# Gated DeltaNet stage: U and transposed W prepared per chunk, the outputs in their own stream, and one block inversion per group

## The chip, the cores and the metric

One core of one Trainium2 chip runs the whole program in one launch. The metric is device time in microseconds (us) of one execution; smaller is better. "Before" is the kernel as it stood, "after" the changed one.

## What is computed

Two layers of a backbone work on 256 context and 256 latent tokens of width 2048. Layer 0 is a bidirectional chunked gated DeltaNet with 16 key heads and 32 value heads, layer 1 a differential attention. The change is in layer 0 alone (and in buffer counts that both layers share). For one chunk of a value head the reference is

```python
lower = jnp.where(strict, jnp.einsum('nbhid,nbhjd->nbhij', kb, kc) * decay, 0.0)
tinv = lax.linalg.triangular_solve(eye + lower, eye, left_side=True, lower=True, unit_diagonal=True)
u = tinv @ (vc * bc[..., None])
w = tinv @ (kb * jnp.exp(gc)[..., None])
def step(s, inp):
    v_new = u_i - w_i @ s
    o_i = q_i @ s + a_i @ v_new
    s = s * gl_i[..., None, None] + jnp.einsum('bhck,bhcv->bhkv', k_i, v_new)
```

Each direction walks over the chunks; the state `s` is carried from step to step, while `tinv`, `u`, `w` and `a_i` depend on no state.

## The kernel before

Tokens lie in four chunks of 128 (two of context, two of latent tokens; a "half" is a pair of them). A group `g` (16 of them) is one key head with its two value heads. Every group needs six projections of 128 columns (q, k, v0, v1, z0, z1), each 16 x 3 matmuls of 512 columns with a weight split into a high and a low part: `raw_tile` loads 128x512 floats by a DMA of the SP queue, ACT casts the high part (L185), POOL or DVE subtracts for the low part (L187). All later stages load their weights through the same `raw_tile` ring (tag `raw`, 4 buffers).

The order of the DeltaNet stage is written by a small planner (`Drive`): generators ("streams") yield their cost on the matmul engine, events or buffer counts, and of the streams that are ready the one of lowest priority number goes on. A scheduler of the framework then places the instructions on the engines' queues; on the chip each queue is in order. The streams are

- `filler` (priority 9): the projections, in the order z0 g, z1 g, q g+1, v0 g+1, v1 g+1, k g+2. What follows a projection (`post_k`, `post_q`, `post_v`, `post_z`) makes the convolution on DVE (L472) and transposes.
- `stream_m` (6): for each half the matrix `ma` (L687 to L748) from a product of the keys and the decay; `grm` is loaded by DMA (L681), scaled by four DVE instructions, exponentiated by ACT. Then `block_inv` (L698): the half's 8 matrices go to memory (`mb_d`), come back as 64 blocks of 16x16 on 64 partitions (`bk`), are inverted row by row with 15 pairs of DVE instructions (`bP` L712, `bY` L714) and go back through `tu_d`.
- `stream_lev` (1.5, two of them): three doubling levels (L777 to L802) from the 16x16 blocks to the inverse `uf` of the whole chunk, with PSUM tag `iv`, DVE result `R` (L783) and ACT casts.
- `stream_at` (5): the decayed product of queries and keys `at`, with loads `gra`.
- `stream_b` (1): four steps t per group, both directions in each. `steps_b` (L849) is one serial chain: keys times state (`sb`), `y` on DVE (L874), a bf16 cast `yb` on ACT (L879), `uf` times `yb`, cast `x0`, `m16` and `ml` times `x0`, a residual on DVE (L905), `uf` times it, `x` (L911), `kx` times `x`, the new state `S` (L918, L921); and in the same step the output `O` from queries times state and `at` times `x`, PSUM tag `so` with one buffer.
- `chain_fin` (2): norm, transposes back and gate `sz` of the outputs. `stream_ada` (7): modulation vectors on POOL and ACT (L138, L139) with loads `aw` and `cr`.

After the groups follow the output projection (`woA`, `woB`), layer 1 with values `dv`, keys `dk`, queries `dq`, gates `dg` for 8 heads, and its output projection `dwo`. Queries, gates and `dwo` have 256 columns per matmul, all else 512.

Of the kernel before, what the change touches and what calls it, by code (L numbers as in the profile page):

```python
# [61 lines left out]
def body(ctx, tc, D, d, out):  # L62
# [87 lines left out]
    def ada_pieces(lcs):  # L150
# [78 lines left out]
    mb_d = [dram.tile([8, US], F16, name=f"mb_d{i}") for i in range(2)]  # L229
    tu_d = [[dram.tile([8, US], F16, name=f"tu_d{i}{j}") for j in range(2)] for i in range(2)]  # L230
# [21 lines left out]
    gq = lambda: pt_("gq", 1)  # L252
# [4 lines left out]
    def so():  # L257
        return psm.tile([P, 2, 2, P], F32, tag="so", name="so", bufs=1)
# [37 lines left out]
    for k0 in range(0, KT, SK):  # L296
        with tc.high_priority():
            for kind in range(2):
                if k0 + kind:
                    pr = kind * HKT + k0 // 2  # L300
                    ada_pair(0, pr, ada_load(0, pr, t0, "ar", 12), (gq, tr)[np_ % 2](), t0)
                np_ += 1
# [24 lines left out]
    lv = cst.tile([P, 3, P], F32, name="lv")  # L327
    nc.sync.dma_start(lv, d["consts"][:, C_LV + 4 * P:C_LV + 7 * P].rearrange("p (l i) -> p l i", l=3))
# [37 lines left out]
    hh = lambda kt: hhi[:, kt, :]  # L366

# [7 lines left out]
    def gates():  # L375
        class t1:
            @staticmethod
            def tile(shape, dt, name, tag, bufs=2):
                return dl.tile(shape, dt, name="gt_" + name, tag=tag, bufs=dict(at=3, x=1, cy=1, jk=1, y=1, grm=1, gra=1, ma=1).get(tag, bufs))
# [53 lines left out]
        g = t1.tile(sh, F32, name="g", tag="x")  # L433
# [57 lines left out]
    def ev(*k):  # L491
        return evs.setdefault(k, Event())

    res = {k: Res(n) for k, n in dict(pj=2, th=2, kT=3, qT=3, v=3, sz0=2,
                                      sz1=2, gq=1, m=4, uf=8, at=3).items()}
# [59 lines left out]
    def post_k(g, ps):  # L555
# [27 lines left out]
        sts[g].update(kT=kT, ktok=kt_)  # L583
        yield 0.87, 1.5 * LX
        dr.set("kT", g)

    def post_q(g, ps):
# [13 lines left out]
        yield 0.0, 9.0 * LX  # L601
        pq = tr()
# [5 lines left out]
        dr.set("rq", g)  # L608
        yield 0.85, 0.0
# [13 lines left out]
    def post_v(g, h, ps):  # L623
        if h == 0:
            yield ("v", 2)
            sts[g]["v"] = [dl.tile([P, 2, 2, P], F32, tag="v", name=f"v{g}{i}", bufs=3) for i in range(2)]
# [9 lines left out]
        v = sts[g]["v"]  # L636
        pv = tr()
# [54 lines left out]
    def scaled(o, gr, pg, s, nm):  # L692
        gm = dl.tile([P, 2, P], F32, tag="gm", name=f"gm{s}{nm}", bufs=1)
        nc.vector.tensor_tensor(gm, pg.unsqueeze(1).to_broadcast([P, 2, P]), gam[:, s], ALU.mult)
# [3 lines left out]
    def block_inv(g, half, m16):  # L698
        par = half
        nm = f"{g}{half}"  # L700
        nc.sync.dma_start(full(mb_d[par]), m16.rearrange("p d c h i -> p (d c h) i"))
        bk = dl.tile([64, 16, 16], F16, tag="bk", name=f"bk{nm}", bufs=1)
# [592 lines left out]
```

## Time and profile before

| | |
|---|---|
| median of 3 runs | 3165.09 us (3162.82 to 3166.16) |
| the profiled execution | 3170.24 us, its span 3168.5 us |
| busy: PE, DVE, ACT, POOL | 89%, 62%, 59%, 64% |
| mean granted clock of TensorE | 0.954 |

PE is the matmul engine, DVE VectorE, ACT ScalarE, POOL GpSimd, SP the queue that issues nearly all DMAs. A busy share of PE counts a matmul until its result is written, so that PE can be 89% busy and still not be issuing at its peak. The page cuts the span into slices: the DeltaNet stage is about the first two thirds (to some 2130 us), the output projection lasts to some 2447 us, layer 1 fills the rest. In the first stage all four engines are half to nine tenths busy, in the last one PE alone is.

### The profile page before, as it was taken

How to read it: one execution, taken by the hardware profiler on the slowest of the kernel's cores; microseconds unless marked ns; L12 is line 12 of the kernel's file. 1: busy time of each engine (PE TensorE's matmuls, PEld its weight loads, DVE VectorE, ACT ScalarE, POOL GpSimd, SP SyncE). 2: the span in 40 equal slices, each digit the busy share in tenths (PEclk: the TensorE clock that was granted, in tenths of full speed). 3: DMA queues.
4: the chain of work that ended last, by engine and by line, in shares of the span. 5: the costliest groups of instructions: out<-in, count | busy, mean ns of one | idle time of the engine just before them, and what ended most of it. 6: DMA issues, size and time to landing. Idle time of an engine off the chain costs nothing.

```text
span 3168.5 us, 52448 instructions
## 1 busy us (share of the span) xinstructions
PE 2833.0 (89%) x16178; PEld 2236.6 (71%) x16178; DVE 1980.1 (62%) x4274; ACT 1863.0 (59%) x5466; POOL 2026.2 (64%) x2370
## 2 busy tenths in 40 slices
PE   4977888888998988998988988899898999999998
PEld 1555666676776766776766766677686888888888
DVE  2148768778778688588688688632334664545454
ACT  3545666666766766766666666654455665434354
POOL 2567677777787777777777777566466677322234
PEclk6988999999999999999999999999999999999999
DMA  9645445455545555545455546656744454333345
GB/s 362 223 114 118 123 119 135 123 133 118 139 134 129 127 126 133 128 129 136 122 125 131 132 118 134 173 171 189 230 147 132 144 164 150 123 110 113 117 127 164
DMA packets 511795, 457.06 MB, mean 144 GB/s; under 512 B 241684, under 2 KB 383764, under 8 KB 511508
## 3 DMA queue, kind: packets, MB, share of 16 engines
q1 hardware_dynamic: 511508, 453.68, 51.8%
q8 instruction: 127, 2.08, 0.3%
q14 instruction: 156, 1.28, 0.1%
q10 hardware_dynamic: 4, 0.02, 0.0%
HBM read 427.18 MB, written 26.36 MB: 143 GB/s over the span
## 4 chain that ended last, share of the span: by engine, by line
PE 33%; DVE 26%; DMA 19%; ACT 7%; POOL 7%; issue 5%; SPq 2%; POOLq 0%; DVEq 0%; ACTq 0%
PE pj L83 28%; DMA gra<-gc_d 5%; POOL rp L138 4%; DMA grm<-gc_d 4%; DVE bP L712 4%; DVE grm L687 3%; DMA aw<-in_adaw_dram 3%; DVE gra L687 2%; DVE bY L714 2%; ACT rp L139 2%; DVE R L783 1%; PE sb L83 1%; DMA ar<-in_adaw_dram 1%; PE iv L83 1%; DVE ma L695 1%
## 5 line engine op out<-in xcount | busy, mean ns | idle before, releaser
L139 ACT ACTIVATE rp<-rp 128x256 f32<-128x256 f32 x1024 | 426.9, 417 | 378.6 <-POOL rp L138 375.5
L712 DVE TENSOR_TENSOR bP<-bX,bY 64x1 f32<-64x1 f32 (+14 forms) x480 | 228.8, 477 | 18.1 <-ACT bY L710 9.8
L139 ACT ACTIVATION_READ_ACCUMULATOR rp<-rp 128x1 f32 x1024 | 194.0, 189 | 0.0
L687 DVE TENSOR_SCALAR gra<-gra,gct,lnb 128x128 f32<-128x128 f32 x256 | 114.3, 488 | 97.9 <-DMA gra<-gc_d 97.2
L687 DVE TENSOR_SCALAR grm<-grm,gct,lnb 128x128 f32<-128x128 f32 x256 | 144.9, 610 | 47.9 <-DMA grm<-gc_d 47.3
L783 DVE TENSOR_TENSOR R<-iv,lv 128x512 f16<-128x512 f32 x192 | 126.1, 678 | 32.8 <-PE iv L83 32.6
L689 ACT ACTIVATE grm<-grm 128x512 f32<-128x512 f32 x64 | 40.4, 631 | 132.0 <-DVE grm L687 127.1
L83 PEld LDWEIGHTS <-m 128*128 128x128 f16 x1024 | 74.2, 100 | 62.0 <-issue 57.7
L714 DVE TENSOR_REDUCE bY<-bP 64x1 f32<-64x1 f32 (+14 forms) x480 | 108.8, 227 | 8.7
L83 PE MATMUL iv<-U,R 128*128 128x128 f16 x768 | 75.7, 223 | 34.4 <-DVE R L783 30.0
L83 PEld LDWEIGHTS <-R 128*128 128x128 f16 x768 | 47.6, 99 | 77.6 <-DVE R L783 44.6
L745 POOL TENSOR_TENSOR ma<-ma,cs 128x512 f32<-128x512 f32 x64 | 85.3, 1333 | 20.7 <-DVE ma L695 18.3
L83 PE MATMUL sb<-yb,uf 128*128 128x128 bf16 x512 | 54.2, 225 | 40.7 <-ACT yb L879 22.2
L689 ACT ACTIVATE gra<-gra 128x512 f32<-128x512 f32 x64 | 40.4, 631 | 84.1 <-DVE gra L687 84.1
L83 PE MATMUL iv<-T,m 128*128 128x128 f16 x768 | 71.4, 223 | 15.8 <-ACT T L800 7.2
L224 DVE TENSOR_TENSOR hlo<-mh,hhi 128x512 fp32r<-128x512 f32 x32 | 29.6, 929 | 86.8 <-ACT hhi L223 77.8
L748 POOL TENSOR_TENSOR ml<-ma,m 128x512 bf16<-128x512 f32 x64 | 76.1, 1189 | 10.5 <-ACT m L747 10.3
L83 PEld LDWEIGHTS <-uf 128*128 128x128 f16 x512 | 36.4, 100 | 64.6 <-issue 59.1
L801 ACT CAST U<-iv 128x512 f16<-128x512 f32 x128 | 75.7, 591 | 0.0
L800 ACT CAST T<-iv 128x512 f16<-128x512 f32 x128 | 73.7, 576 | 3.0 <-PE iv L83 2.9
L83 PE MATMUL so<-x,at 128*128 128x128 f32 x512 | 71.6, 280 | 3.8 <-DVE x L911 2.7
L83 PEld LDWEIGHTS so<-x,at 128*128 128x128 f32 x512 | 64.9, 194 | 6.2 <-DVE x L911 3.6
(2758 smaller groups left out, 11429.3 us busy)
## 6 DMA issues: line engine op xcount, KB each, us to landing
aw<-in_adaw_dram SPq DMA_DIRECT2D x512, 128.0 KB, 3.0
ar<-in_adaw_dram SPq DMA_DIRECT2D x64, 512.0 KB, 7.3
gra<-gc_d SPq DMA_DIRECT2D x128, 128.0 KB, 4.2
grm<-gc_d SPq DMA_DIRECT2D x128, 128.0 KB, 4.1
mb_d<-m SPq DMA_DIRECT2D x32, 256.0 KB, 3.7
T<-tu_d SPq DMA_DIRECT2D x128, 64.0 KB, 2.7
U<-tu_d SPq DMA_DIRECT2D x128, 64.0 KB, 2.7
yd<-sz SPq DMA_DIRECT2D x32, 256.0 KB, 3.4
```

The lines of the kernel that those rows point to most:

```text
L83: nc.tensor.matmul(o, l, r, start=start, stop=stop)
L138: nc.gpsimd.tensor_tensor(pr, r, cr[:, s], ALU.mult)
L139: nc.scalar.activation(pr, pr, AF.Copy, accum_out=acc[:, s, q:q + 1])
L687: nc.vector.tensor_scalar(gr[:, u], gr[:, u], gct[:, c, dd, j:j + 1], lnb[:, c, dd, j:j + 1], ALU.subtract, ALU.min)
L689: nc.scalar.activation(gr, gr, AF.Exp)
L712: nc.vector.tensor_tensor(pr[:, :i, :i], X[:, i, :i].unsqueeze(1).to_broadcast([64, i, i]), Y[:, :i, :i].rearrange("p j c -> p c j"), ALU. ...
L714: nc.vector.tensor_reduce(Y[:, i, :i], pr[:, :i, :i], AX.X, ALU.add)
L745: nc.gpsimd.tensor_tensor(ma, ma, ident.unsqueeze(1).to_broadcast([P, 4, P]), ALU.add)
L748: nc.gpsimd.tensor_tensor(ml[:, :, k], mv, m16[:, :, k], ALU.subtract)
L783: nc.vector.tensor_tensor(R, quad(pp), lvb(n), ALU.mult)
L800: nc.scalar.copy(Tm, quad(pt))
L801: nc.scalar.copy(U, quad(pu))
```

## The change

- `block_inv(g)` is called once per group, after the second half's `ma`: 128 blocks on 128 partitions instead of 64 on 64, the same 15 pairs of DVE instructions. Both halves of `m16` go to one `mb_d`.
- `stream_v` (1.7) makes U = inverse times v for each chunk (product, correction by `m16` and `ml`, second product: 16 small matmuls a chunk, as `steps_b` had). `stream_w` (1.6) makes W transposed for each chunk and direction but those of step 0: `ek` on POOL, a bf16 cast, then 10 small matmuls (two heads: 2, 4, 4), a DVE residual and ACT copies, six times per group.
- `steps_b` keeps W times state, `x -= b`, `kx` times `x` and the state. `stream_o` (1.3) makes the outputs.
- `masked` multiplies both chunks' product by the mask in one DVE instruction and frees the PSUM bank early.
- Buffers: `raw` 4 to 3, `cr` 2 to 1, `m16` and `ml` 4 to 3, `v` 3 to 2, `uf` 8 to 4, `kT` 3 to 2; `so` 1 to 2 in PSUM, for which the tag `gq` shares the one bank of `tr`.

```diff
-        r = wp.tile([P, 512], F32, tag="raw", name=nm, bufs=4)
+        r = wp.tile([P, 512], F32, tag="raw", name=nm, bufs=3)
...
+    MB, VB, UFB, UB, WB, CRB = 3, 2, 4, 2, 3, 1
...
-    gq = lambda: pt_("gq", 1)
+    gq = tr
...
-        return psm.tile([P, 2, 2, P], F32, tag="so", name="so", bufs=1)
+        return psm.tile([P, 2, 2, P], F32, tag="so", name="so", bufs=2)
...
-    def block_inv(g, half, m16):
+    def block_inv(g):
...
-        X = dl.tile([64, 16, 16], F32, tag="bX", name=f"bX{nm}", bufs=1)
+        X = dl.tile([P, 16, 16], F32, tag="bX", name=f"bX{g}", bufs=1)
...
-                sts[g].setdefault("tu", []).append(block_inv(g, half, m16))
+                for dd in range(2):
+                    u = 8 * dd + 4 * half
+                    nc.sync.dma_start(full(mb_d[g % 2])[:, u:u + 4], m16[:, dd].rearrange("p c h i -> p (c h) i"))
+                if half == 1:
+                    sts[g]["tu"] = block_inv(g)
...
+    def stream_v():
...
+                    for dd, h in DH:
+                        mm(b[:, dd, h], uf[:, 2 * dd + h], vb[:, h])
+                    x0 = dl.tile([P, 2, 2, P], BF16, tag="x0", name=f"x0{g}{c}", bufs=1)
+                    nc.scalar.copy(x0, b)
...
+                    for dd, h in DH:
+                        mm(b[:, dd, h], m16[:, dd, k, h], x0[:, dd, h], True, False)
+                        mm(b[:, dd, h], ml[:, dd, k, h], x0[:, dd, h], False, True)
+                    rb = dl.tile([P, 2, 2, P], BF16, tag="vb", name=f"rb{g}{c}", bufs=1)
+                    nc.vector.tensor_tensor(rb, v[:, k].unsqueeze(1).to_broadcast([P, 2, 2, P]), b, ALU.subtract)
...
+                    for dd, h in DH:
+                        mm(b[:, dd, h], uf[:, 2 * dd + h], rb[:, dd, h])
+                    us = U[:, 0:4:3] if k == 0 else U[:, 1:3]
+                    nc.vector.tensor_tensor(us, x0, b, ALU.add)
...
+                free("v")
+                done("m", ("m", g, half), 2)
...
+    def stream_w():
...
+                    for i, dd in enumerate(dds):
+                        nc.gpsimd.tensor_tensor(ek[:, i], ktok[:, c].unsqueeze(1).to_broadcast([P, 2, P]),
+                                                eg[:, c, dd, 2 * g:2 * g + 2].unsqueeze(2).to_broadcast([P, 2, P]),
+                                                ALU.mult)
+                    eb = dl.tile([P, nd, 2, P], BF16, tag="eb", name=f"eb{g}{c}", bufs=1)
+                    nc.scalar.copy(eb, ek)
...
+                    for i, dd, h in N:
+                        mm(b[:, i, h], x0[:, i, h], idh, True, False)
+                        mm(b[:, i, h], rb[:, i, h], uf[:, 2 * dd + h], False, True)
+                    for i, dd in enumerate(dds):
+                        t = 2 * half + (k if dd == 0 else 1 - k)
+                        nc.scalar.copy(W[t][:, dd], b[:, i])
...
         if t > 0:
+            W = st["W"][t]
             b = sb()
...
             for dd, h in DH:
+                mm(b[:, dd, h], W[:, dd, h], S[:, dd, h])
+            nc.vector.tensor_tensor(x, x, b, ALU.subtract)
...
+    dr.add(1.3, stream_o())
+    dr.add(1.7, stream_v())
+    dr.add(1.6, stream_w())
```

The next two pieces show the matmul queue (PE) at a state update, before and after. In both, `pj` is a projection (`g12k` is the k projection of group 12), `sb` and `so` belong to the chain and the outputs, `tr` to transposes. Before, in group 10's chain:

```order
L83 MATMUL pj<-hhi,g12khi_17979 128x512
L83 MATMUL pj<-hlo_1187,g12khi_17979 128x512
L83 MATMUL so<-S_17047,qT_15802 128x256 x2
L83 MATMUL pj<-hhi,g12klo_17980 128x512
L83 MATMUL pj<-hhi,g12khi_18017 128x512
L83 MATMUL pj<-hlo_1329,g12khi_18017 128x512
L83 MATMUL pj<-hhi,g12klo_18018 128x512
L83 MATMUL pj<-hhi,g12khi_18017 128x512
```

The product of queries and state stands between projections, as all other work does: from group 3 on no run between two matmuls of projections has more than 33 matmuls. After, the end of what stands between the projections z0 and z1 of group 10:

```order
L660 MATMUL tr<-cs,thg10v_16922 128x128 x4
L1094 MATMUL so<-cs,O_15951 128x128 x3
L83 MATMUL so<-S_16398,qT_14821 128x256 x2
L1094 MATMUL so<-cs,O_15951 128x128
L83 MATMUL tr<-qT_16421,kT_15866 128x128 x2
L83 MATMUL sb<-U_16286,kx_16873 128x128 x4
L83 MATMUL pj<-hhi,g10z1hi_17335 128x512
L83 MATMUL pj<-hlo_279,g10z1hi_17335 128x512
```

From the last matmul of z0 to the first of z1 there are 96 rows with 176 matmuls and not one projection among them: U and W of a half, two state updates, transposes and outputs have moved there. Groups 2 to 14 have such a run ahead of z1, of 72 to 192 matmuls.

On DVE, the rows behind the state update of step 1 (`S`, L1018 of the changed file) in the same place of the changed program; the 15th row behind these is the `x -= b` of step 2 (L1002), for which the last matmuls of that run wait:

```order
L1018 SCALAR_TENSOR_TENSOR S_16398<-S_16271,egl,sb 128x128 x4
L948 TENSOR_TENSOR rk_16371<-ek_16255,so 128x512
L1050 SCALAR_TENSOR_TENSOR O_15951<-so,eg,O_15951 128x128 x4
L721 TENSOR_TENSOR at_16514<-gra_16506,gm_16494 128x512
L1062 TENSOR_TENSOR O_15951<-O_15951,so 128x512
L716 TENSOR_TENSOR gm_16572<-tr,cs 128x512
L893 TENSOR_TENSOR rb_16535<-v_15361,so 128x512
L721 TENSOR_TENSOR ma_16582<-grm_16574,gm_16572 128x512
L709 TENSOR_SCALAR gra_17175<-gra_17175,gct,lnb 128x128 x2
L948 TENSOR_TENSOR rk_16555<-ek_16461,so 128x512
L709 TENSOR_SCALAR gra_17175<-gra_17175,gct,lnb 128x128 x2
L95 TENSOR_SCALAR rs_t<-tr 128x4
```

What used to be spread over a group (residuals, masks, decays of other streams) now stands between one state update and the next.

## Rows read from the trace of the kernel before

**Rows 1.** The profile's page, its first line.

```profile
span 3168.5 us, 52448 instructions
```

**Rows 2.** One stretch: length; PE, PEld, DVE, ACT, POOL busy; clock; DMA share; GB/s.

```profile
451.00:1753.00 1302.00, 1160.06 (x6818) 895.38 (x6817) 1018.57 (x2356) 859.55 (x2675) 981.78 (x1212) 0.96 0.52 130
```

**Rows 3.** One tile's instructions: duration min/median/max ns, first and last start us.

```profile
L83 PE MATMUL pj<-hhi,g2z0hi x16: 392/394/482, 451.0 to 474.5; 128*128 128x512 f32 x16
...
L83 PE MATMUL pj<-hhi,g13z0hi x16: 392/398/502, 1753.1 to 1771.4; 128*128 128x512 f32 x16
```

**Rows 4.** Groups by line, 451 to 1753 us: busy us, mean ns, idle before.

```profile
L712 DVE TENSOR_TENSOR bP<-bX,bY 64x1 f32<-64x1 f32 (+4 forms) x354 | 166.6, 471 | 12.0 <-ACT bY L710 6.0
...
L687 DVE TENSOR_SCALAR grm<-grm,gct,lnb 128x128 f32<-128x128 f32 x192 | 111.7, 626 | 34.8 <-DMA grm<-gc_d 34.6
...
L687 DVE TENSOR_SCALAR gra<-gra,gct,lnb 128x128 f32<-128x128 f32 x188 | 83.8, 487 | 71.7 <-DMA gra<-gc_d 71.1
...
L714 DVE TENSOR_REDUCE bY<-bP 64x1 f32<-64x1 f32 (+4 forms) x354 | 79.7, 225 | 6.0
...
L865 POOL TENSOR_TENSOR kx<-ktok,kd 128x256 f32<-128x256 f32 x70 | 47.1, 693 | 0.9 <-PE sb L83 0.9
...
L874 DVE SCALAR_TENSOR_TENSOR y<-sb,eg,v 128x128 f32<-128x128 f32 x136 | 38.5, 338 | 4.1 <-PE sb L83 3.9
...
L694 DVE TENSOR_TENSOR gm<-gq,cs 128x256 f32<-128x256 f32 x93 | 38.5, 414 | 3.4 <-PE gq L83 2.5
...
L911 DVE TENSOR_TENSOR x<-x,sb 128x512 f32<-128x512 bf16 x46 | 31.0, 675 | 13.2 <-PE sb L83 9.8 <-ACT cyg8q L467 3.4
...
L898 ACT CAST x<-sb 128x512 bf16<-128x512 f32 x45 | 26.0, 578 | 2.1 <-PE sb L83 2.0
```

**Rows 5.** The chain that ended last in 451 to 1753 us, shares by line.

```profile
by line: PE pj L83 12.6%; DMA gra<-gc_d 8.6%; DMA grm<-gc_d 7.4%; DVE bP L712 6.9%; DVE grm L687 6.3%; issue 4.2%; DVE gra L687 4.1%; DVE R L783 2.9%; DVE bY L714 2.9%; POOL rp L138 2.5%; DMA bk<-mb_d 2.1%; DMA aw<-in_adaw_dram 2.0%; DVE ma
```

**Rows 6.** Who waited for whom, PE alone, 451 to 1753 us: total us, times, longest.

```profile
PE iv L83 <- DVE R L783: 23.2, 25, 3.7
...
PE sb L83 <- ACT yb L879: 14.1, 12, 3.6
```

**Rows 7.** Instructions of PE in order of time: start us, us, what.

```profile
1077.05 0.40 PE L83 MATMUL pj<-hlo,g7z1hi 128*128 128x512 f32 x1
1077.29 0.40 PE L83 MATMUL iv<-R,U 128*128 128x128 f16 x4
...
1077.81 0.39 PE L83 MATMUL pj<-hhi,g7z1hi 128*128 128x512 f32 x1
...
1086.35 0.83 PE L83 MATMUL sb<-x,kx 128*128 128x128 f32 x6
1087.01 0.61 PE L83 MATMUL iv<-T,m 128*128 128x128 f16 x8
```

**Rows 8.** A long wait of PE, and the stretch behind it (columns as in Rows 2).

```profile
953.75 0.59 PE L83 MATMUL sb<-yb,uf 128*128 128x128 bf16 x4 [3.56 <-ACT yb L879]
...
953.80:960.50 6.70, 5.95 (x25) 4.18 (x24) 4.04 (x14) 6.15 (x25) 4.29 (x7) 0.50 0.54 104
```

**Rows 9.** The SP queue in order of time, L119 loads of the last stage.

```profile
3090.21 5.42 SPq L119 DMA_DIRECT2D dwo6r<-in_dawo_dram  x4
...
3124.05 5.03 SPq L119 DMA_DIRECT2D dwo12r<-in_dawo_dram  x4
```

**Rows 10.** DMA issues: count, KB each, median us from issue to landing.

```profile
dq40r<-in_daw_dram SPq DMA_DIRECT2D x4, 256.0 KB, 3.0
...
dwo6r<-in_dawo_dram SPq DMA_DIRECT2D x4, 256.0 KB, 3.9
```

**Rows 11.** The split of a loaded tile in the last stage (columns as in Rows 3).

```profile
L185 ACT CAST dwo5hi<-dwo5r x4: 620/622/623, 3088.3 to 3093.3; 128x512 fp32r<-128x512 f32 x4
L187 DVE TENSOR_TENSOR dwo5lo<-dwo5r,dwo5hi x2: 694/969/1244, 3088.9 to 3091.7; 128x512 fp32r<-128x512 f32 x2
L187 POOL TENSOR_TENSOR dwo5lo<-dwo5r,dwo5hi x2: 1293/1296/1298, 3090.1 to 3094.0; 128x512 fp32r<-128x512 f32 x2
```

More of the change, by code (lines that the diff above doesn't have):

```diff
@@ L378, in tile @@
             def tile(shape, dt, name, tag, bufs=2):
-                return dl.tile(shape, dt, name="gt_" + name, tag=tag, bufs=dict(at=3, x=1, cy=1, jk=1, y=1, grm=1, gra=1, ma=1).get(tag, bufs))
+                return dl.tile(shape, dt, name="gt_" + name, tag=tag, bufs=dict(at=3, kx=1, cy=1, jk=1, y=1, grm=1, gra=1, ma=1).get(tag, bufs))
         if NB < P:
@@ L492, in ev, with done @@
         return evs.setdefault(k, Event())
-    res = {k: Res(n) for k, n in dict(pj=2, th=2, kT=3, qT=3, v=3, sz0=2,
-                                      sz1=2, gq=1, m=4, uf=8, at=3).items()}
+    res = {k: Res(n) for k, n in dict(pj=2, th=2, kT=2, ktok=3, qT=3, v=VB, sz0=2,
+                                      sz1=2, gq=1, m=MB, uf=UFB, at=3, U=UB, W=WB, so=2).items()}
+    cnt = {}
+    def done(what, key, n):
+        cnt[key] = cnt.get(key, 0) + 1
+        if cnt[key] == n:
+            free(what)
     class Drive:
@@ L625, in post_v @@
             yield ("v", 2)
-            sts[g]["v"] = [dl.tile([P, 2, 2, P], F32, tag="v", name=f"v{g}{i}", bufs=3) for i in range(2)]
+            sts[g]["v"] = [dl.tile([P, 2, 2, P], F32, tag="v", name=f"v{g}{i}", bufs=VB) for i in range(2)]
             dr.set("vt", g)
@@ L729, in stream_m @@
                 yield ("gq", 1)
-                if g > 0:
-                    for p in range(2):
-                        yield ev("ld", g - 1, half, p)
+                if g > 1 and half == 0:
+                    for hf in range(2):
+                        for p in range(2):
+                            yield ev("ld", g - 2, hf, p)
                 nm = f"{g}{half}"
-                m16 = dl.tile([P, 2, 2, 2, P], F16, tag="m16", name=f"m16{nm}", bufs=4)
-                ml = dl.tile([P, 2, 2, 2, P], BF16, tag="ml", name=f"ml{nm}", bufs=4)
+                m16 = dl.tile([P, 2, 2, 2, P], F16, tag="m16", name=f"m16{nm}", bufs=MB)
+                ml = dl.tile([P, 2, 2, 2, P], BF16, tag="ml", name=f"ml{nm}", bufs=MB)
                 pg = gq()
@@ L749, in stream_m @@
                 sts[g].setdefault("m", []).append((m16, ml))
-                sts[g].setdefault("tu", []).append(block_inv(g, half, m16))
-                dr.set("tu", g, half, lat=32)
-                free("gq", 1, 14)
+                for dd in range(2):
[3 more added lines that the diff above has]
+                    sts[g]["tu"] = block_inv(g)
+                    for hf in range(2):
+                        dr.set("tu", g, hf, lat=32)
                 yield 0.44, 12.0 * LX
+            done("kT", ("kT", g), 2)
     def stream_lev(p):
@@ L827, in stream_b @@
+    DH = [(dd, h) for dd in range(2) for h in range(2)]
     def stream_b():
@@ L923, in steps_b @@
[L923 to L933 removed]
+            mm(b[:, dd, h], kx[:, dd, h], x[:, dd, h])
+        Sn = vec("S", bufs=2)
```

320 lines of the change are left out of this document (202 added, 118 removed).

## The prediction

> **What bounds the kernel now.** I read the windows first. The stretch from 451 to 1753 us is 1302 us of the span of 3168.5 [rows 1, 2]; the z0 projection of group 2 starts at its beginning and that of group 13 at its end [rows 3], so it holds 11 groups of 118.4 us. In it PE is busy for 1160 us, idle for 142, which is 12.9 a group; DVE for 1018.6, 92.6 a group [rows 2]. So PE bounds the stage, with a ninth of it lost. Who loses it stands in PE's waits: `iv` for the DVE residual `R` (23.2 us), `sb` for the ACT cast `yb` (14.1 us) [rows 6]. Neither is large by itself; the chain says why they come late: matmuls of the projections hold 12.6%, a row of DVE work and its loads far more (`bP` 6.9, `bY` 2.9, `grm` 6.3, `gra` 4.1, the loads `gra` and `grm` 8.6 and 7.4, `bk` 2.1) [rows 5]. The groups by line show the same on DVE: it stands idle for 71.1 and 34.6 us for the two loads, and `bP` with `bY` takes 246 us [rows 4]. The reader is to see an in-order DVE queue that is late here and there, and a PE that is nearly full wherever DVE is on time.
>
> **The change, part by part.** Sixteen groups; each term is a group's price times the groups.
>
> *One inversion instead of two.* `bP` and `bY` are 354 each for 11 groups (two times 15 a group, with an edge), 166.6 + 79.7 us [rows 4]. On 128 partitions a row of the inversion should take what it takes on 64, so half goes: 246.3/11/2 = 11.2 us of DVE a group. On the chain they are 6.9 + 2.9 = 9.8% of 1302 us = 128, or 11.6 a group [rows 5]; half is 5.8. The reload `bk` (2.1%, 27 us) halves too, 1.2. I take 7.0 x 16 = **-112**. Bounds: nothing, if the chain turns to other DVE work; 12.6 x 16 = -202, if all DVE time that goes (11.2 here, 1.4 more below) comes off the end.
>
> *DVE else.* `y` goes, 38.5/11 = 3.5 a group; three `x -= b` come, priced as `x` at 0.675, 2.0; W's residuals (two of full, two of half width, 0.675 and 0.414 as `gm`) are 2.2; the joined mask saves 0.8 (four of 512 columns for eight of 256), and the rest of the inversion (`bX`), halved too, some 1.3, an estimate from its share of the instructions. With the inversion that is -12.6 a group and DVE at 80; it is in the bound above and not counted twice.
>
> *The cast `yb` leaves the chain.* PE's wait for it is 14.1 us in 11 groups, 1.3 each [rows 6]: **-21**. Bounds: 0, if what follows waits as long, and -21.
>
> *W's 60 small matmuls a group.* A step of four 16-bit ones between two projections moves the next from 0.24 to 0.76 us later: 0.76 less two spacings of 0.23 is 0.30, 0.07 each; six fp32 ones take 0.66, 0.11 each [rows 7]. Sixty are 4.2 us a group, 67 in all. Some two thirds stand in the run of the next term, where PE waits anyway, so I take 1.4 x 16 = **+22**; bounds 0 and +67.
>
> *The run without projections.* The order shows it: in groups 2 to 14 the last matmuls ahead of z1 need the `x -= b` of step 2. Behind the state update of step 1 DVE has first: 8 scaled additions (0.338 as `y`), 15 operations of 512 (0.675 as `x`), 4 `grm` (0.626), 4 `gra` (0.487), 2 of 256 columns (0.45, near `gm`), then that `x -= b`: 2.7 + 10.1 + 2.5 + 1.9 + 0.9 + 0.7 = 18.8 us [rows 4]. PE's own work there, at 0.07 and 0.11, is 4.8 to 11.6 us, mostly some 9.3 [rows 7]. Nothing else is queued on PE, so it waits 18.8 - 9.3 = 9.5 in each of 13 runs: **+125**. Bounds: 0, if DVE has done most of these before the update (they are independent of it, but the queue is in order), and +180, if the wait for a load of `grm` or `gra` stands in it too (105.7/11 = 9.6 us a group are so spent now [rows 4]; I allow 4 in a run). The first end is why faster keeps a third of the chances.
>
> *POOL and ACT.* Six `ek` at 0.693 (as `kx`) are 4.2 us of POOL [rows 4], on a queue that is busy for 981.8 of 1302 [rows 2]. ACT loses 9 casts and gets 18, 14 of them of half size: at 0.578 for a full one [rows 4] and between half and all of that for a small one, +1.2 to +5.2 a group. ACT and POOL have a third and a quarter of their time left [rows 2]. What hides this is PE's own work; where it doesn't, R of the levels comes later. I take 1.0 a group, **+16**; bounds 0 and, with all of both (3 + 4.2), +115.
>
> *Three `raw` buffers.* Every later stage loads through this ring. In the last one 24 loads (`dwo6r` to `dwo12r`, four each) are 33.84 us apart, 1.41 each [rows 9]. A buffer is busy from issue to the end of its split: landing 3.0 to 3.9 us (I take 3.3) [rows 10], cast 0.62, subtraction 0.69 to 1.30, typically 0.97 [rows 11], with some 0.2 between, 5.1. Four buffers give one in 1.28 us, under the 1.41 that PE needs; three give one in 1.70. That is 0.29 for each of 64 loads, 18; the queries and gates have the same 256 columns a matmul but more work beside, which I estimate at 0.5 for each of 8 heads: **+23**. Bounds: +6 with landing at 3.0 and the quick split (4.5/3 = 1.5), +76 with landing at 3.9 and the slow split on POOL (6.0/3 = 2.0, 38 for `dwo` and as much for the queries and gates). Stages of 512 columns need a tile half as often and are hidden by PE.
>
> *The clock.* Now it is 0.96 in the stretch [rows 2]. Behind a wait of 3.56 us on `yb` it stood at 0.50, the lower of the two levels, for 6.7 us [rows 8]; half of that is lost, 3.3. If each run brought one such wait the 13 would cost 43 more. I take 0, as the small matmuls of the chain and of W cut the wait into pieces. The Trainium skill ("TensorE: Matmul & The Clock Gate", "HAM oscillation") says that an engine that waits between bursts of matmuls is throttled again and starts each burst cold. By it the sum would be 43 higher; the row agrees for one long wait, and no row shows many short ones.
>
> *The other buffers.* The single `cr` and the shared `tr` bank delay off-path work; `uf`, `v`, `kT` are released earlier by the new streams. I cost them at nothing; the cover is the work of the next group, and where `m16` fails to give it, the third rival speaks.
>
> Sum: -112 - 21 + 22 + 125 + 16 + 23 = **+53**. The profiled execution took 3170.24 us, 5.15 above the median of 3165.09; 3170.24 + 53 = 3223, on the median **3218 us**.
>
> **The rivals.** *Faster (chance 0.31).* DVE, relieved by 12.6 us a group, runs ahead of PE and has the independent work behind it when the update comes. Then a run costs 3 us at most (39) and the ring 8 instead of 23: -112 - 21 + 22 + 39 + 8 = some -61 after leaving POOL and ACT's 16 at 3, so 3104, its own range 3040 to 3150. For it: DVE idles 9.6 us a group for loads alone; against it: the order puts the residuals of both later chunks into the run, and these wait for PE's own products.
>
> *No change (0.08).* The run gives back just what the inversion saves, 3159 to 3171; 0.2% or 6.3 us is about what a measurement of this kernel can tell.
>
> *The ring `m16` decides (0.11), slower.* With three buffers half 1 of the next group waits until U and W of half 0 are done, and its inversion can start only then. From there to the next such point stand the inversion with its two trips to memory, three levels, U and W, in series; from the rows I estimate 85 us (inversion 11, `ma` and loads 30, the rest levels and waits). It decides from 118.4 us up; at 127, half as long again as my estimate, each group costs 8.6 more than now: 3165 + 16 x 8.6 = 3303. Against it: 85 leaves 33 us.
>
> *U and W don't run ahead.* That the new streams don't do what they are called for is part of the forecast: those of the second half stand inside the run, between the updates.
>
> *The clock falls in every run (0.12):* as behind the long wait of [rows 8], 3218 + 43 = 3261, in the upper part of the forecast's range. Against it: only one such wait is shown.
>
> **How the numbers follow.** The forecast has 0.38, with 3180 to 3300 as its own range, in which the clock's 0.12 lies; with the ring's 0.11 slower has 0.61, same 0.08, faster 0.31. From 3085, which leaves out about a third of the faster case, to 3310, which leaves out half of the ring's, some 0.18 lies outside.
>
> **What would show it.** `bP` and `bY` at 15 each a group with unchanged means; PE's waits ahead of z1 at some 10 us a group, released by DVE (`x -= b`, S), with DVE full there; the distance from group 2 to group 13 up from 1302 us by some 40 (11 runs of 9.5, and 11/16 of the -95 of the other terms of the stage); `dwo` loads 1.7 us apart instead of 1.41 with ACT's casts waiting for DMA; the clock near 0.95. It is wrong if DVE has idle time in the run ahead of z1, if `bP` on 128 partitions costs more than 0.471, if the loads keep 1.41, or if the order of waits is led by `m16`.

## The result: 9% slower, and the profile after

The changed kernel takes 3456.64 us (median of 4 runs, 3454.57 to 3460.38), the kernel before 3164.05 beside it: ratio 1.0925, 95% interval 1.0906 to 1.0944. That is +292 us where the prediction had +53, and outside its range. The page of the profiled execution begins with these lines (DVE had 62% before, POOL 64%):

```profile
span 3456.5 us, 54735 instructions
...
PE 2983.8 (86%) x17330; PEld 2358.5 (68%) x17330; DVE 1811.2 (52%) x3618; ACT 1898.1 (55%) x5612; POOL 2031.7 (59%) x2466
```

The first matmuls of named tiles cut each profiled span into stretches (us; the experiments named in the other columns come below):

| | before | after | b_cr1 | b_raw3 | a_cr2r4 | a_wcut |
|---|---|---|---|---|---|---|
| start to z0 of group 2 | 451.0 | 465.7 | 454.8 | 452.0 | 465.6 | 460.7 |
| 11 groups, to z0 of group 13 | 1302.1 | 1445.1 | 1337.0 | 1307.9 | 1396.5 | 1336.8 |
| to `woA0` | 260.6 | 302.1 | 267.2 | 255.4 | 284.6 | 256.2 |
| output projection and `dv`, to `dk00` | 482.7 | 540.9 | 518.3 | 487.2 | 518.1 | 498.2 |
| rest of layer 1, to `dwo0` | 556.8 | 570.7 | 591.9 | 571.8 | 548.5 | 554.9 |
| `dwo` to the end | 115.3 | 132.0 | 116.7 | 132.0 | 115.3 | 114.5 |

So 143 us of the loss lie in the 11 groups that [rows 3] bound, 42 in the stretch behind them, and 58 in the output projection with the values `dv` behind it (54 in the projection itself), for which the prediction had nothing. The 11 groups after, as [rows 2] had them before (length; PE, PEld, DVE, ACT, POOL busy; clock; DMA share; GB/s), and the tiles that bound them:

```profile
465.70:1910.80 1445.10, 1233.19 (x7470) 960.41 (x7469) 864.19 (x1792) 892.97 (x2833) 1010.18 (x1315) 0.94 0.47 119
...
L83 PE MATMUL pj<-hhi,g2z0hi x16: 392/394/484, 465.7 to 481.1; 128*128 128x512 f32 x16
...
L83 PE MATMUL pj<-hhi,g13z0hi x16: 392/394/477, 1910.8 to 1925.1; 128*128 128x512 f32 x16
```

A group takes 131.4 us instead of 118.4. PE is busy for 73 us more and idle for 212 instead of 142, 19.3 a group instead of 12.9; DVE is busy for 154 us less. The same groups of lines as [rows 4], 466 to 1911 us:

```profile
L709 DVE TENSOR_SCALAR grm<-grm,gct,lnb 128x128 f32<-128x128 f32 x180 | 95.9, 576 | 82.1 <-DMA grm<-gc_d 81.8
...
L709 DVE TENSOR_SCALAR gra<-gra,gct,lnb 128x128 f32<-128x128 f32 x172 | 72.1, 461 | 74.2 <-DMA gra<-gc_d 73.7
...
L735 DVE TENSOR_TENSOR bP<-bX,bY 128x1 f32<-128x1 f32 (+4 forms) x165 | 68.1, 413 | 3.5
...
L925 POOL TENSOR_TENSOR ek<-ktok,eg 128x256 f32<-128x256 f32 x65 | 40.1, 632 | 5.5 <-DVE rk L948 5.4
...
L737 DVE TENSOR_REDUCE bY<-bP 128x1 f32<-128x1 f32 (+4 forms) x165 | 38.9, 236 | 3.6
...
L948 DVE TENSOR_TENSOR rk<-ek,so 128x256 bf16<-128x256 f32 (+1 forms) x44 | 24.1, 547 | 22.5 <-PE so L83 19.4 <-ACT x L884 2.5 <-PE pj L83 0.2
...
L1002 DVE TENSOR_TENSOR U<-U,sb 128x512 f32<-128x512 f32 x33 | 22.4, 680 | 17.5 <-PE sb L83 17.4
```

The inversion is 165 pairs in 11 groups instead of 354, and a pair of steps on 128 partitions costs no more than one on 64 (0.413 + 0.236 us beside 0.471 + 0.225). DVE is relieved by 14.0 us a group where the prediction said 12.6, and the time got longer all the same. PE's waits, as [rows 6]:

```profile
PE so L83 <- DVE rb L893: 18.5, 14, 2.5
PE iv L83 <- DVE R L815: 17.1, 16, 2.6
PE so L83 <- DVE rk L948: 14.0, 10, 2.6
PE iv L83 <- DMA T<-tu_d: 13.2, 7, 4.5
PE sb L83 <- ACT W L958: 11.9, 8, 2.7
```

Three of the five are links of the new chains (`rb` of U, `rk` and the copy of W); `R` and the load `T` were there before. None is large by itself. The run of matmuls without a projection that the order showed is there in all of groups 2 to 14: z0 of group 10 ends and z1 starts 30 us later; in between PE is busy for 20 of 30 us, at a clock of 0.83.

```profile
L83 PE MATMUL pj<-hhi,g10z0hi x16: 393/397/483, 1511.9 to 1526.3; 128*128 128x512 f32 x16
...
L83 PE MATMUL pj<-hhi,g10z1hi x16: 392/398/586, 1556.7 to 1571.3; 128*128 128x512 f32 x16
...
1527.00:1556.70 29.70, 20.14 (x158) 17.14 (x156) 20.19 (x44) 20.01 (x66) 20.98 (x29) 0.83 0.38 106
```

Inside it, in order of time, PE stands for `xk`, then for `rk`, two links of W's chain; z1 itself comes when DVE has read the bank of the next k projection (`cyg11k`):

```profile
1539.69 0.22 PE L83 MATMUL so<-x,m 128*128 128x128 bf16 x1 [2.73 <-ACT xk L939]
1539.74 0.22 PE L83 MATMUL so<-x,ml 128*128 128x128 bf16 x1
...
1543.98 0.26 PE L83 MATMUL so<-idh,xk 128*128 128x128 bf16 x1 [1.75 <-DVE rk L948]
...
1554.94 1.06 PE L83 MATMUL sb<-U,kx 128*128 128x128 f32 x8
1556.69 0.51 PE L83 MATMUL pj<-hhi,g10z1hi 128*128 128x512 f32 x1 [0.70 <-DVE cyg11k L479]
```

In the 11 such runs of groups 2 to 12 PE waits for 84 us in all. By releaser, summed over the trace: `rk`, the copy of W and `xk` 34.5, `rb` 10.4, the state `S` 10.1, the `x -= b` of which the prediction made the whole wait 3.2.

On POOL, in order of time, the product `rp` of the modulation waits 3.48 us for its `cr`. Behind it in the queue stand W's `ek` and the low part of g11z0, and PE (the last line) waits 1.81 us for that low part.

```profile
1644.20 0.74 POOL L187 TENSOR_TENSOR g11z0lo<-g11z0r,g11z0hi 128x256 fp32r<-128x256 f32 x1
1648.43 0.74 POOL L138 TENSOR_TENSOR rp<-aw,cr(1, 16)7_27221 128x256 f32<-128x256 f32 x1 [3.48 <-DMA cr(1, 16)7_27221<-sc_d]
1649.13 1.18 POOL L925 TENSOR_TENSOR ek<-ktok,eg 128x256 f32<-128x256 f32 x2
1650.27 0.72 POOL L187 TENSOR_TENSOR g11z0lo<-g11z0r,g11z0hi 128x256 fp32r<-128x256 f32 x1
...
1651.05 0.50 PE L83 MATMUL pj<-hhi,g11z0lo 128*128 128x512 f32 x1 [1.81 <-POOL g11z0lo L187]
```

### The profile page after: what moved, and what is told of

Same layout as the page of the kernel before. It is cut to its first block, busy times and chain, and to the rows that moved or that the text cites. A ratio compares the mean times of both kernels' runs of the same rounds, so it can differ in the third digit from the quotient of the medians.

```text
span 3456.5 us, 54735 instructions
## 1 busy us (share of the span) xinstructions
PE 2983.8 (86%) x17330; PEld 2358.5 (68%) x17330; DVE 1811.2 (52%) x3618; ACT 1898.1 (55%) x5612; POOL 2031.7 (59%) x2466
## 5 line engine op out<-in xcount | busy, mean ns | idle before, releaser
L709 DVE TENSOR_SCALAR grm<-grm,gct,lnb 128x128 f32<-128x128 f32 x256 | 132.0, 560 | 116.9 <-DMA grm<-gc_d 116.3
L709 DVE TENSOR_SCALAR gra<-gra,gct,lnb 128x128 f32<-128x128 f32 x256 | 103.1, 444 | 120.7 <-DMA gra<-gc_d 120.0
L83 PEld LDWEIGHTS <-m 128*128 128x128 f16 x1216 | 96.9, 102 | 74.3 <-issue 71.2
L735 DVE TENSOR_TENSOR bP<-bX,bY 128x1 f32<-128x1 f32 (+14 forms) x240 | 104.0, 433 | 5.0
L83 PE MATMUL iv<-T,m 128*128 128x128 f16 x768 | 74.9, 226 | 29.6 <-DMA T<-tu_d 14.1
L83 PE MATMUL sb<-S,W 128*128 128x128 f32 x384 | 67.7, 319 | 31.6 <-ACT W L958 16.0
L83 PEld LDWEIGHTS <-uf 128*128 128x128 f16 x704 | 53.0, 108 | 60.1 <-issue 45.9
L83 PE MATMUL so<-U,at 128*128 128x128 f32 x512 | 77.5, 292 | 8.8 <-DVE U L1002 3.3
L83 PEld LDWEIGHTS sb<-S,W 128*128 128x128 f32 x384 | 58.9, 222 | 37.7 <-ACT W L958 19.2
L83 PEld LDWEIGHTS so<-U,at 128*128 128x128 f32 x512 | 69.1, 203 | 13.3 <-DVE U L1002 5.2
L901 DVE TENSOR_TENSOR U<-x,so 128x512 f32<-128x512 bf16 x64 | 43.6, 681 | 65.5 <-PE so L83 53.7
```

Source lines behind the costliest of these rows:

```text
L83: nc.tensor.matmul(o, l, r, start=start, stop=stop)
L709: nc.vector.tensor_scalar(gr[:, u], gr[:, u], gct[:, c, dd, j:j + 1], lnb[:, c, dd, j:j + 1], ALU.subtract, ALU.min)
L735: nc.vector.tensor_tensor(pr[:, :i, :i], X[:, i, :i].unsqueeze(1).to_broadcast([P, i, i]), Y[:, :i, :i].rearrange("p j c -> p c j"), ALU.mult)
L901: nc.vector.tensor_tensor(us, x0, b, ALU.add)
```

## The experiments

Every run has the kernel before beside it on its chip, and ratios are to that one; differences of ratios are turned into us of 3165 (0.001 is 3.2 us). Each experiment changes one or two things of before (b_) or after (a_).

**The prediction's terms by themselves.** In before, three `raw`; one `cr`; the inversion as in the change, with its buffers and the index of the levels' loads:

```diff
-        r = wp.tile([P, 512], F32, tag="raw", name=nm, bufs=4)
+        r = wp.tile([P, 512], F32, tag="raw", name=nm, bufs=3)      # b_raw3
-            cr = wp.tile([P, 2, NK], F32, name=f"cr{lcs[0]}{q}", tag="cr", bufs=2)
+            cr = wp.tile([P, 2, NK], F32, name=f"cr{lcs[0]}{q}", tag="cr", bufs=1)      # b_cr1
...
-                sts[g].setdefault("tu", []).append(block_inv(g, half, m16))
...
+                if half == 1:
+                    sts[g]["tu"] = block_inv(g)      # b_inv
...
```

> The kernel before with one number changed: three raw buffers instead of four. My prediction charged the ring 23 us, all in the last stage. The changed kernel lost 288 us of span: 199 by the end of the groups, 54 in the output projection, 35 in layer 1. Theory A (the raw ring makes both late losses): 3164 + 70 to 90 = some 3245, with 54 of it in the output projection. Theory B (the raw ring costs only what I charged, the output projection suffers from something else): 3164 + 20 to 35 = some 3190, the output projection unchanged, dwo loads 1.6 to 1.7 us apart.

> The kernel before with one number changed: one cr buffer instead of two. My prediction charged nothing. Theory A (a cr load that waits for its only buffer stands at the head of the SP queue and holds the raw loads behind it): the output projection and the gaps beside late modulation work lose some 50, total 3164 + 40 to 80 = some 3220. Theory B (cr is off the path): 3164 within 10.

> The kernel before with the inversion alone changed to once per group on 128 partitions, all buffers as before. By the prediction's term: 3164 - 112 = 3052, DVE less by 11 us a group. Rival (the levels of the first half now start only after the second half's matrices, the matmul queue waits for that and the saving goes): 3155 to 3200, DVE less all the same. In between (half the term): some 3110.

b_raw3: 3218.56, ratio 1.0161 (1.0132 to 1.0190), 51 us, between the two theories. Its profiled execution was the fastest of the four, 38 us over before; 32 of these lie in layer 1 and `dwo`, 4.5 in the output projection with `dv`. b_cr1: 3290.29, ratio **1.0390** (1.0371 to 1.0409), 123 us for one buffer of 2 KB a partition. b_inv: 3174.05, ratio 1.0019 (1.0005 to 1.0033): nothing won. Its 11 groups:

```profile
463.70:1752.60 1288.90, 1149.33 (x6771) 897.05 (x6769) 889.52 (x1924) 831.78 (x2609) 954.83 (x1212) 0.96 0.52 130
...
L710 DVE TENSOR_TENSOR bP<-bX,bY 128x1 f32<-128x1 f32 (+4 forms) x165 | 75.0, 455 | 3.5
...
L712 DVE TENSOR_REDUCE bY<-bP 128x1 f32<-128x1 f32 (+4 forms) x165 | 38.7, 234 | 3.4
```

DVE is busy for 889.5 us instead of 1018.6, 11.7 less a group. The 11 groups are 13 us shorter, where the prediction's term makes 77 of them, and the stretch ahead of them is 13 us longer (463.7 instead of 451.0). PE idles for 140 us in them instead of 142, and its first wait is still the one for DVE's `R`, 29.0 us (23.2 before [rows 6]). The edit does one thing more, named as the rival in its expectation: the levels of the first half can't start before the second half's matrices. No run takes the saving and this delay apart.

The rows of POOL's waits that b_cr1 has and before hasn't (waiting, releaser: us, times, longest):

```profile
POOL rp L138 <- DMA cr(1, 24)7_27696<-sc_d: 5.1, 1, 5.1
...
POOL rp L138 <- DMA cr(1, 16)4_26180<-sc_d: 5.0, 1, 5.0
```

Summed over the whole trace (each `cr` tile has a row of its own), `rp` waits for `cr` 229.6 us in 102 waits there, and 253.6 in 108 in the changed kernel; the kernel before has no such wait.

**The same in the changed kernel.** Room for a second `cr` comes from a smaller `bX` (16 bits) and shared tags. a_cr2r4 adds a fourth `raw` buffer in a pool opened when the groups' buffers are gone. a_actq leaves one `cr` and changes the queue of the loads; b_actq does this in before:

```diff
-    MB, VB, UFB, UB, WB, CRB = 3, 2, 4, 2, 3, 1
+    MB, VB, UFB, UB, WB, CRB = 3, 2, 4, 2, 3, 2      # a_cr2, a_cr2r4
+            r = rp_[0].tile([P, 512], F32, tag="raw4", name=nm, bufs=1)      # a_cr2r4, every fourth load
-        nc.sync.dma_start(r, d["adaw"][l, ct, :, q * NK:(q + 1) * NK])
+        nc.scalar.dma_start(r, d["adaw"][l, ct, :, q * NK:(q + 1) * NK])      # a_actq, b_actq; cr alike
```

> The changed kernel with two cr buffers again; the room comes from bX in 16 bits, bk in the tag of bP and a setup tile under another tag. One cr buffer cost the kernel before 122 us. Theory A (the same head-of-line wait of the SP queue is what the changed kernel loses, and adds to the rest): 3457 - 90 to 130 = some 3340, the output projection back from 487 to some 440, the rows of SP waiting at L158 for POOL gone. Theory B (in the changed kernel the groups are held by the new streams, which hide the wait): 3457 - 50 at the most, all of it behind the groups.

> As a_cr2, and a fourth raw buffer from the end of the first half of the output projection on (after the groups' buffers are gone). Theory A: three raw buffers cost the kernel before 51 us, 38 of them behind the groups, so this is 25 to 40 under a_cr2, the dwo loads again some 1.4 us apart. What then stands between it and 3165 belongs to the new streams of the groups: by adding up, 292 - 122 - 40 = some 130. Theory B (the rings do not add): within 10 of a_cr2.

> The changed kernel as it is (one cr, three raw buffers); only the loads of the modulation weights aw and of cr are issued by ACT's queue instead of SP's. With two cr buffers the changed kernel gained 98 us. Theory A (the price of the single cr is the SP queue: a load that waits for its buffer holds grm, gra, tu and raw loads behind it): the same is won without a buffer, 3457 - 70 to 110 = some 3365. Theory B (the single buffer slows the modulation work itself, POOL waiting for cr): 3440 or more, perhaps slower, as ACT now issues 600 loads.

> The kernel before with the same move of the aw and cr loads to ACT's queue. SP waits 217 us for POOL at the aw loads in 451 to 1753 us. Theory A (these waits delay other loads on the path there too): 3165 - 15 to 60. Theory B (with two cr buffers they are covered): 3165 within 15.

a_cr2: ratio **1.0571** (1.0548 to 1.0594), that is 0.0354 or 112 us under the changed kernel; a_cr2r4: 1.0494 (1.0471 to 1.0517), another 24. a_actq: 1.0838 (1.0820 to 1.0856), 28 us; b_actq: 0.9997 (0.9985 to 1.0009), so the move to ACT's queue by itself costs nothing. The smaller `bX` is not what gives the 112: a_vb3 and a_th3 below have it too, use the room for another buffer and gain 10 and 13. The waits around the modulation, first in the changed kernel, then in a_cr2:

```profile
POOL rp L138 <- ACT rp L139: 231.8, 269, 4.5
...
POOL rp L138 <- DMA cr(0, 36)5_8011<-sc_d: 6.9, 2, 3.8
...
POOL rp L138 <- DMA cr(1, 0)6_20096<-sc_d: 6.6, 1, 6.6
POOL rp L138 <- DMA cr(1, 36)5_32527<-sc_d: 6.5, 1, 6.5
...
ACT rp L139 <- POOL rp L138: 622.1, 577, 6.8
...
SPq L158 <- POOL rp L138: 140.8, 95, 6.7
```

```profile
POOL rp L138 <- ACT rp L139: 331.9, 341, 4.4
...
POOL rp L138 <- DMA cr(0, 32)1_2511<-sc_d: 5.0, 1, 5.0
...
POOL rp L138 <- DMA cr(0, 32)0_2334<-sc_d: 1.7, 1, 1.7
...
ACT rp L139 <- POOL rp L138: 374.2, 473, 5.4
```

In a_cr2 the two rows shown are all that is left of the waits for `cr`, 6.7 us; POOL waits more for ACT instead. So theory A on a_cr2 holds in its size, and its mechanism in part at most. SP's queue did stand for POOL at the `cr` loads (L158, 140.8 us; a_cr2 has no such row), but taking the loads out of that queue won only 28 of the 112, and left `rp` 210.7 us of waits in 98. The larger part goes, by what is left over, to the compute queues: with one buffer a load isn't issued before the last product of the old `cr` is done, POOL then stands until it has landed, and the splits of the projections stand behind it. ACT, which adds up each product, stands with POOL: it waits 622 us for `rp` instead of 374 in a_cr2, with the casts of the projections in its queue.

How this reaches PE can be read in part: its waits for low parts made by POOL (L187), summed over the trace, are 33 us in before and 75 in b_cr1, 70 in the changed kernel and 40 in a_cr2. And the waits have no fixed price: 247 us less of `rp` waiting for `cr` went with 112 us (a_cr2), 43 less with 28 (a_actq).

**What sets the run without projections.** a_vb3 and a_th3 have one more buffer for `v` or `th`, in the room that a_cr2 uses; a_gq1 returns the masked products' bank and takes it from `so`:

```diff
+    MB, VB, UFB, UB, WB, CRB = 3, 3, 4, 2, 3, 1      # a_vb3
+        th = dl.tile([P, T], F32, tag="th", name=f"th{nm}", bufs=3)      # a_th3, and its count in the planner
-    gq = tr
+    gq = lambda: pt_("gq", 1)      # a_gq1, with
+        return psm.tile([P, 2, 2, P], F32, tag="so", name="so", bufs=1)
```

> The changed kernel with three v buffers instead of two; room for it comes from a setup tile under another tag, bX as 16-bit and bk in the tag of bP. Theory A (v of the next group waits for U of this one, so the convolutions hold both banks of the projections, z1 cannot start and the matmul queue runs dry for 16 to 32 us ahead of it): with the ring wider the run ahead of z1 shrinks under 10 us and a group from 131.4 to some 120, total 3457 - 150 to 200 = some 3280. Theory B (the run is held by other things: the scratch ring th, the shared transpose bank, or the serial chains of U and W): run still 16 to 32 us, 3457 within 20.

> The changed kernel with three th scratch buffers (same room as in a_cr2, here used for th). In its trace z1 starts when the convolution of the next k leaves its projection bank, and that one waits for a th. Theory A (th is what holds the bank): the run without projections shrinks, a group from 131.4 to 122 or less, 3457 - 100 or more. Theory B (a wider ring only moves the run behind the next projection; the new chains of small matmuls set its length): a run of 15 to 30 us stands between z1 and the next q instead, total 3457 within 30.

> The changed kernel with the masked products in a bank of their own again, for which the outputs, U and W share one bank (so 1 instead of 2). Theory A (the shared transpose bank delays the transposes of v and so the projections): 3457 - 50 or more. Theory B (the bank of so is what the new streams need; U, W and the outputs take turns on one): longer runs, 3457 + 20 to 100.

a_vb3: 1.0893 (1.0864 to 1.0923). a_th3: 1.0883 (1.0857 to 1.0910). a_gq1: **1.1907** (1.1878 to 1.1935). A break is a stretch of over 8 us between two matmuls of projections. In the 11 groups the breaks add up to 320 us in the changed kernel (16 breaks), 233 in a_vb3 (11) and 215 in a_th3 (10, now between z1 and the next q): some 30% less, for 10 and 13 us. So as long as the single `cr` is there, the breaks have hardly a price of their own. The bank of `so` has one: U, W, outputs and final transposes on one bank cost 0.098 (311 us) more than on two, though the masked products have theirs back.

**What W costs.** b_mm60 puts 60 small matmuls a group into before, with nobody to read them; a_wcut takes W's correction out of a_cr2r4, a_w0 all of W:

```diff
+            ex = so()      # b_mm60, in the steps 1 to 3
+            for i in range(20):
+                dd, h = DH[i % 4]
+                mm(ex[:, dd, h], uf[cd[dd]][:, 2 * dd + h], yb[:, dd, h])
...
-                        mm(b[:, i, h], m16[:, dd, k, h], x0[:, i, h], True, False)      # a_wcut: from x0 to the sum
-                        mm(b[:, i, h], rb[:, i, h], uf[:, 2 * dd + h], False, True)
-                        mm(b[:, i, h], uf[:, 2 * dd + h], eb[:, i, h])      # a_w0: this too
+                        nc.scalar.copy(W[t][:, dd], eb[:, i])
```

> The kernel before with 20 more small 16-bit matmuls in each of the steps 1 to 3 of every group (60 a group, 960 in all), whose products nobody reads; they stand where the outputs stand. The price of W's matmuls by itself. By my 0.07 us each, all of it on the path: 3165 + 67 = 3232. What the prediction took for the stage (two thirds hidden): + 22. If the wait for the bank they use adds to it: + 90 or more.

> As a_cr2r4 (3337), but W is the first product alone: its correction is left out (40 of the 60 matmuls a group, the DVE residual and the cast between them), so the outputs differ by rounding. Theory A (W's matmuls are paid for in full): 40 x 0.07 x 16 = 45 less, 3290. Theory B (the chain of W, not its work, sets the length of the run without projections): 80 or more less, the runs under 15 us. Theory C (the run is set by U and the state updates): within 15 of a_cr2r4.

> As a_wcut (ratio 1.018), but W is left out altogether: a copy of the scaled keys stands in its place, so no matmul, no bank and no wait for W is left (the outputs are not the reference's). What U ahead, the outputs in their own stream, the shared bank and the one inversion give without W's cost. Theory A (W was the rest of the loss): 20 matmuls a group and one bank use less, ratio 0.99 to 1.01. Theory B (the rebuilt streams lose by themselves, above all in the first groups): 1.01 to 1.02, the stretch from g1z0 to g2z0 still some 150 us instead of 120.

b_mm60: ratio 1.0143 (1.0126 to 1.0160), 45 us for 960 matmuls, 0.047 each; its 11 groups:

```profile
455.40:1801.60 1346.20, 1191.97 (x7468) 937.89 (x7467) 1007.01 (x2342) 872.04 (x2734) 991.94 (x1242) 0.96 0.53 128
```

PE is busy for 32 us more there. a_wcut: ratio **1.0178** (1.0156 to 1.0200), 100 us under a_cr2r4, where the 640 matmuls left out are worth 30 by b_mm60. The rest goes with the chain (two products, two evictions, two turns on a bank fewer for each W): the breaks add up to 74 us (3) instead of 284 (15) in a_cr2r4, and behind z0 of group 10 there is none; z0 and z1 take 19 us each instead of 14.5, since other work lies between their matmuls again (17 and 18 us in before).

```profile
L83 PE MATMUL pj<-hhi,g10z0hi x16: 393/397/628, 1440.1 to 1459.7; 128*128 128x512 f32 x16
...
L83 PE MATMUL pj<-hhi,g10z1hi x16: 392/394/776, 1461.2 to 1480.0; 128*128 128x512 f32 x16
...
460.70:1797.50 1336.80, 1175.65 (x7070) 914.96 (x7068) 870.33 (x1774) 857.00 (x2717) 984.97 (x1274) 0.96 0.50 125
```

a_w0 came out slower than a_wcut, 1.0258 (1.0235 to 1.0281), outside both theories, with 9 breaks of 188 us together. Less work came out slower; the planner and the scheduler make the whole order anew for every kernel, and nothing else was found. So a difference of some 0.008 between two kernels can't be read as the price of an edit, and how far above that an order by itself can move the time was not tried.

**What is left.** v in 16 bits with four buffers (a_cr2r4v4), this with W's correction out (a_wcutv4), and the shared bank by itself (b_gqtr):

```diff
-            sts[g]["v"] = [dl.tile([P, 2, 2, P], F32, tag="v", name=f"v{g}{i}", bufs=VB) for i in range(2)]
+            sts[g]["v"] = [dl.tile([P, 2, 2, P], BF16, tag="v", name=f"v{g}{i}", bufs=VB) for i in range(2)]      # VB = 4
-    gq = lambda: pt_("gq", 1)
+    gq = tr      # b_gqtr
```

> As a_cr2r4 (ratio 1.049 to the kernel before), with v in 16 bits and four buffers for it instead of two (the same bytes), so that v of the next group never waits for U. Theory A (with the cr wait gone, the v ring is what holds the run without projections): ratio 1.02 to 1.03, runs under 15 us. Theory B (runs are set by the chains of W and U on their two banks, as the kernel without W's correction suggests): ratio within 0.01 of a_cr2r4.

> Both cuts together: two cr, four raw buffers late, v in 16 bits with four buffers, and W without its correction. Alone, v's buffers took the ratio from 1.049 to 1.032 (55 us, 52 of them between g1z0 and g2z0), W's correction from 1.049 to 1.018 (100 us). Theory A (they are two losses, the start and the groups): ratio 0.998 to 1.005, so that cr, raw, v and W's correction are the whole loss of the change. Theory B (both lift the same stall): 1.012 to 1.018, and some 45 us stay with the rebuilt streams.

> The kernel before with the masked products in the transposes' bank (one bank for both, the other left unused). What the sharing costs by itself, which my prediction charged at nothing. Theory A (it delays the matrices and the convolutions): 3165 + 30 to 80. Theory B (nothing, the bank is read quickly): 3165 within 15.

a_cr2r4v4: 1.0320 (1.0305 to 1.0336), 55 us under a_cr2r4; 52 are won between the z0 of group 1 and that of group 2 (102.5 us instead of 154.5), none in the 11 groups. a_wcutv4: 1.0168 (1.0140 to 1.0197), as theory B had it: nothing under a_wcut, and 48 us under a_cr2r4v4. So the two don't add: W's correction is worth 100 us with two buffers for `v` and 48 with four. 0.0168 or 53 us remain with the rebuilt streams. b_gqtr: **0.9929** (0.9909 to 0.9948), a gain of 22 us against both theories.

**Parts of the change alone, in before.** b_invmix inverts once per group in groups 3 to 13 alone; b_gqmix adds the shared bank:

```diff
+    HG, TG = 3, 2      # b_invmix, b_gqmix
...
+                if g < HG or g >= G - TG:
+                    sts[g]["tu"] = block_inv(g, half)
...
+                elif half == 1:
+                    sts[g]["tu"] = block_inv(g)
```

> The kernel before with the inversion once per group in groups 3 to 13 and once per half in groups 0 to 2, 14 and 15. The single inversion alone came out even (3174 beside 3168), but in its profile the 11 middle groups took 1288.9 us instead of 1302.1, and the stretch before them 12.7 more. Theory A (the middle wins, the start and the end lose): 3165 - 10 to 20, faster than both kernels. Theory B (the difference of the stretches is chance between two schedules): 3165 within 8.

> The kernel before with the two parts of the change that won alone: the masked products in the transposes' bank (ratio 0.993) and the inversion once per group in groups 3 to 13 (0.998). Theory A (they add): 0.991, some 3140. Theory B (each only drew another schedule, and a third is drawn here): 0.990 to 1.000 with no relation to the two.

b_invmix: 0.9979 (0.9967 to 0.9990), 7 us, within theory B; b_gqmix: 0.9976 (0.9963 to 0.9989). Their sum, 0.991, isn't there: theory B. b_gqtr, 3149.76 beside 3169.78, is the fastest that was run, faster than both kernels; why sharing a bank helps was not found, and the 0.007 is no more than a new order can be worth by a_w0.

## Why the prediction was wrong, step by step

- **"I cost them at nothing"**, of the other buffers: the first step that failed, and the one that the runs show alone in both kernels. The single `cr` costs 112 us in the changed kernel and 123 in before. `v`, also in this list, was not free either: a third buffer for it gave 10 us beside the single `cr` (a_vb3), and four of 16 bits gave 55 once `cr` had two (a_cr2r4v4). The text called the modulation off-path work; its product stands in POOL's in-order queue, which also makes the low parts of every projection, and [rows 2] showed that queue three quarters busy. The rule to ask what is queued behind the waiting instruction, used on DVE, was not used here.
- **The inversion, -112:** the second step that failed. The DVE saving was right (11.7 a group in b_inv, 11.2 predicted for the pairs and 1.3 for the rest of the inversion), but in before the edit was worth 0 at the end and 13 us in the 11 groups. The share of the chain in [rows 5] was taken for a price. A chain that is followed back from one end names the releasers along one path; that the next path was as long is the reading here, not shown, and the later start of the first half's levels is the other.
- **W's 60 matmuls, +22:** the third step. By themselves they cost 45 (b_mm60; 67 was the bound). What was missing is W's chain: three products a chunk, each with a bank of `so` and an eviction. Leaving out the correction gave 100, some 70 beyond its matmuls; with four buffers for `v` it gave 48, some 18 beyond them.
- **The run without projections, +125:** it is there in each of the 13 places, and the 11 between groups 2 and 12 leave PE idle for 84 us of 262, 7.6 each against 9.5 predicted (9.5 in 13 runs is 124, written as 125). That the size is near is luck, since the cause is another: the links of W's chain (34.5 of the 84 us) and of U's (`rb` 10.4), not 27 DVE instructions ahead of one `x -= b` (3.2). DVE, which the prediction had full there, idles for 56 of the 262 us, one of its own signs of being wrong. And idle time elsewhere became less: a group has 6.4 us more of it, not 9.5 and more.
- **Three `raw`, +23:** right for the last stage. The `dwo` loads stand 41.18/24 = 1.72 us apart (predicted 1.70, 1.41 before [rows 9]), and `dwo` took 16.7 more where 18 were predicted. A fourth buffer for the late stages gave 24 back. In before, though, three buffers cost 51, twice the term.

```profile
3367.22 5.25 SPq L119 DMA_DIRECT2D dwo6r<-in_dawo_dram  x4
...
3408.40 5.07 SPq L119 DMA_DIRECT2D dwo12r<-in_dawo_dram  x4
```

- **The cast `yb`, -21, and POOL and ACT, +16:** not tried alone. The wait for `yb` is gone, but PE's new waits in the 11 groups are longer than it was (`rb` 18.5 us, `rk` 14.0, W 11.9, against 14.1 [rows 6]). The reading of [rows 6] also passed over PE's second longest wait, 14.8 us for DVE's residual `yb`, of which `rb` is the successor.
- **The clock, 0:** it is 0.94 in the 11 groups instead of 0.96 [rows 2], and 0.75 to 0.92 in the 11 runs, in which PE stands for 7.6 us on average, in several pieces (0.83 in the run shown). So the rival that it falls in every run was right in kind, and that small matmuls between the waits prevent it was wrong. By the ratio of the two means it is 2% of PE's busy 1233 us, some 25 of the 143; an estimate, not tried. The prediction cited the Trainium skill ("TensorE: Matmul & The Clock Gate", "HAM oscillation — how this bites in real kernels") for an engine that waits between bursts of matmuls being throttled again; the 0.75 to 0.92 of these runs agree.
- **The rival `m16`** was not tried by itself; it isn't among the five longest waits of PE above.

Added up in the order of the runs: `cr` 112, `raw` 24, W's correction 100, and 53 not settled, 289 of 292 (the other 3 lie between a_wcut and a_wcutv4). The first is shown in both kernels with nearly one size, the second in both with two (24 and 51); the third overlaps with `v`'s buffers, and another order of the runs would give it 48 and `v` 55. In the 53 are W's first product, the streams of U and the outputs, the clock, and the output projection, which with `dv` takes 518 us instead of 483 even in a_cr2r4 and for which no run found the cause.

## What to carry to other kernels

Before a buffer is taken from a ring (the set of buffers that tiles of one tag take in turn), look at the engine that reads it and at everything that stands behind the reader in its queue, and behind whoever waits for the reader; whether the ring's own work is urgent says nothing. With one buffer the reader's queue stood for the reload in 108 waits here, and that cost 112 us. The share that a line has in the chain of waits is no price: halving a DVE stage that held 10% of the chain moved nothing at the end. And where a scheduler makes the order anew for every kernel, an edit's effect under one per cent needs the edit alone and a control before it gets a cause.

## What was not expected of the hardware

A pair of inversion steps on 128 partitions took no longer than on 64 (0.413 + 0.236 us beside 0.471 + 0.225), so the halving was free on DVE, as assumed. Each wait for a `cr` load cost POOL 2.35 us (253.6/108), which 2 KB a partition of a second buffer had hidden whole. Small 16-bit matmuls cost the program 0.047 us each (45/960), two thirds of what their spacing in one place suggested (0.07 [rows 7]).
